# A hybrid encoder with gathered experts: buffers of the prompt's routing moved off the gather ring's space, the first ids at raised priority, norm products on ScalarE and POOL

## The chip, the cores and the metric

The kernel runs on one core of a Trainium2 chip. The metric is the device time of one execution in microseconds (us); less is better. The kernel before takes 4287.37 us, the median of three runs (4286.51 to 4300.59).

## What is computed

One encoder layer is applied with the same weights to two groups of tokens: the prompt (1 x 256 tokens) and the sample (1 x 1024 tokens), each of width 1024. Cut to what matters here:

```python
h = rmsnorm(x, norm_mix)                       # the "norm" of this case
parts = split(h @ w_in)                        # the projection
y_h = hgrn2_branch(...) @ w_br_h
y_a = mla_branch(...) @ w_br_a
x = x + (sigmoid(gl_h) * y_h + sigmoid(gl_a) * y_a) @ w_out    # the merge
z = rmsnorm(x, norm_ffn)
# PEER: 8 heads, 128 x 128 experts, 16 chosen per head
q = (z @ peer_wq) -> (token, head, 2, 128)
vals, idx = top_k(q . sub_keys, 16)            # per half of the key
top, pos = top_k(sums of the 16 x 16 pairs, 16)
g = softmax(top); e = ids of the chosen experts
act = gelu(z . peer_u[e]) * g                  # 128 rows of 1024 per token
x = x + sum(act * peer_v[e])                   # 128 rows of 1024 per token
y = rmsnorm(x, norm_final)
```

All data are float32. The two tables `peer_u` and `peer_v` have 16384 rows of 1024 each.

## The kernel before

Tokens lie in tiles of 128. The prompt has two tiles, the sample eight. The program goes through the prompt's projection, scan and attention first; then through the norm of the sample (its first step); then through the prompt's `merge`; and then through the sample's projection, scan, attention and merges. For six tiles (two of the prompt, four of the sample) the experts' rows are gathered from DRAM; for the other four of the sample all 16384 experts are multiplied densely on PE, at the end of the program.

The work of the sample's norm is in `project` (L204), loop L212 to L221. For each tile of 128 tokens it loads `xt` (L214), takes the sum of squares (`norm_T`, L187 to L201, squares on ScalarE, the sum over partitions on PE, L198, and the root on ScalarE and DVE, L165 to L171) into `nr`, and then for each of 8 slices of the width makes `hf` = xt x gain x nr in one operation on DVE (L218). `put` (L154) splits it in two parts for PE: ScalarE casts `hh` (L159), DVE subtracts `hl` = hf - hh (L160). `hf` has three buffers. The projection (`block`, `proj`, L138 to L142) multiplies each weight block first with tokens 0 to 511 of the sample and then with tokens 512 to 1023; each matmul is done as three (hh x wh, hl x wh, hh x wl).

The prompt's `merge` (L699) combines the branches, adds x, stores the new rows to `x2d` (L762), and then for 16 blocks of query weights `wq` (j = 0 to 15, L138 with `xg`) copies the result (`qT`, ScalarE, L867), multiplies it with the keys on PE (L871), and takes the best 16 of each on DVE (`best`, L849 to L857). After j = 7 the heads 0 to 3 of a tile have all scores: `half(c, 0)` (L812) makes their 64 ids `ei` (L845). `finish_picks` (after the loop) makes the other half.

The gathers are in `experts`, `u_steps` (L928) and `v_steps` (L951). `u_steps` loads the tile's rows `zs` (on POOL's queue, L931), multiplies by the norm (L934), and then for each of 128 choices gathers 128 rows of `peer_u` (512 KB, issued by POOL, L938) and multiplies them with `zs` on DVE, with the sum over a row kept (L940). `v_steps` gathers rows of `peer_v` (L969), and PE adds four of them at a time to `acc` (L976, 8 matmuls). The gathers go through a ring of seven buffers (`ring`, L925) in a pool that is opened at L1166, together with `zt`, set to zero by POOL at L1169.

Each pool is on the left or the right side of the on-chip memory, and pools of a side are stacked: a pool opened later on the right takes the place of pools closed before. On the right, `wpp` (L1137), the prompt's weight pool, stays open through the prompt's merge, and the merge puts its own pool C (`xg`, `qT`, `ssq`, L710) on the right too; the ring's pool comes after both.

The order of instructions on each engine is fixed when the program is built: a scheduler runs through the program with its own estimates of durations and issues what is ready, by priority; `tc.high_priority()` raises that of the instructions made inside it. On the chip each engine executes its list in order, with semaphores between engines. POOL's list has the gathers, SP's the plain loads and stores.

Of the kernel before, what the change touches and what calls it, by code (L numbers as in the profile page):

```python
# [12 lines left out]
F32 = mybir.dt.float32  # L13
# [5 lines left out]
AF = mybir.ActivationFunctionType  # L19
OP = mybir.AluOpType  # L20
# [22 lines left out]
G_MIX, G_FFN, G_QA, G_KVA, G_HG = 0, 8, 16, 19, 21  # L43
# [7 lines left out]
def encoder(ctx, tc, I, O, dbg=None):  # L51
    nc = tc.nc
# [5 lines left out]
    vsp = vctx.enter_context(tc.tile_pool(name="vs", bufs=1, side="left"))  # L58
    wctx = ctx.enter_context(ExitStack())
    wp = wctx.enter_context(tc.tile_pool(name="wp", bufs=2, side="left"))  # L60
# [6 lines left out]
    gains = const.tile([P, 25], F32, name="gains")  # L67
# [83 lines left out]
        return (pool.tile(shape, F32R, name=name + "h", **{k: v + "h" if k == "tag" else v for k, v in kw.items()}),  # L151
                pool.tile(shape, F32R, name=name + "l", **{k: v + "l" if k == "tag" else v for k, v in kw.items()}))

    def put(dst, src):  # L154

        if len(dst) == 1:
            nc.scalar.copy(dst[0], src)
        else:
            nc.scalar.copy(dst[0], src)  # L159
            nc.vector.tensor_tensor(dst[1], src, dst[0].bitcast(F32), op=OP.subtract)  # L160

    def rsqrt_to(pool, out, src, inv_n, shape, name, vy=None):

# [40 lines left out]
    def project(s0, S, ap, wpool, bank, np_, whole):  # L204
# [5 lines left out]
        H = parts(ap, [P, KD, S], "h", whole)  # L210
        ns = 256 if whole else 128
        for t0 in range(0, S, ns):  # L212
            xt = np_.tile([P, KD, ns], F32, name="xt", tag="xt", bufs=256 // ns)
            nc.sync.dma_start(xt, I["xT"][:, :, s0 + t0:s0 + t0 + ns])  # L214
            r = norm_T(np_, [xt[:, k] for k in range(KD)], KD, ns, "nA", bank, whole)
            for k in range(KD):
                hf = H[0][:, k, t0:t0 + ns] if whole else np_.tile([P, ns], F32, name="hf", tag="hf", bufs=3)
                nc.vector.scalar_tensor_tensor(out=hf, in0=xt[:, k], scalar=gains[:, G_MIX + k:G_MIX + k + 1],  # L218
                                               in1=r, op0=OP.mult, op1=OP.mult)
                if not whole:  # L220
                    put([a[:, k, t0:t0 + ns] for a in H], hf)  # L221
        yield

        def stage():
# [471 lines left out]
        nc.vector.tensor_tensor(j, j, last, op=OP.add)  # L696
        return i, j

    def merge(s0, t0, G, nd, routes, wpool, rp, bank, wb=3, small=False, tbank=None, tside="left", tctx=None, cut=0, sp=None, mp=None):  # L699

        with ExitStack() as own, ExitStack() as cctx:
# [3 lines left out]
            segs = [(a, b) for a, b in ((0, ndt), (ndt, G)) if a < b]  # L707
            if not nd:
                cp = own.enter_context(tc.tile_pool(name=f"T{s0}_{t0}", bufs=1, side=tside))
            ca = cctx.enter_context(tc.tile_pool(name=f"C{s0}_{t0}", bufs=1, side="right"))  # L710
            xs = [ca.tile([P, KD, b - a], F32, name=f"xg{a}") for a, b in segs]
            rt = rp.tile([P, ng], F32, name="rt", tag="rt", bufs=4)
            ssq = ca.tile([P, G], F32, name="ssq")
# [145 lines left out]
            for j in range(16):  # L859
# [15 lines left out]
                    norm()  # L875
                if j == 7:
                    for c in range(nd or 1):
                        half(c, 0)
            if nd:
                for k in range(KD):  # L880
                    z = ca.tile([P, ndt], F32, name="z", tag="qT0", bufs=2)
# [243 lines left out]
    def psum_pool(ctx, name, n, side):  # L1125
        pool = ctx.enter_context(tc.tile_pool(name=name, bufs=n, space=bass.MemoryType.PSUM, side=side))
        return lambda: pool.tile([P, 512], F32, name="pm", tag="pm")

    (p0, PS), (s0, SS) = SEQS
    routes = []  # L1130
    rp = ctx.enter_context(tc.tile_pool(name="rp", bufs=1, side="right"))
# [2 lines left out]


    with ExitStack() as pctx:
        wpp = pctx.enter_context(tc.tile_pool(name="wpp", bufs=1, side="right"))  # L1137
        with ExitStack() as qctx:
            bankA = psum_pool(qctx, "psA", 2, "right")
            bankB = psum_pool(qctx, "psB0", 2, "right")  # L1140
            bankT = psum_pool(qctx, "psT0", 1, "right")
# [20 lines left out]
        prs = project(s0, SS, ap, wp, bankF, np_, False)  # L1162
        next(prs)
        with ExitStack() as mctx:
            merge(p0, 0, PS, 0, routes, wpp, rp, psum_pool(mctx, "psM0", 4, "right"), small=True, cut=1, sp=wp, mp=vsp)
    pe_ = ctx.enter_context(tc.tile_pool(name="peer", bufs=1, side="right"))  # L1166
    zts.append(pe_.tile([P, 2, 4, 4, 32], F32, name="zt0"))
    for z_ in zts:
# [51 lines left out]
    tctx = ExitStack()  # L1220
# [95 lines left out]
```

## Time and profile before

| | |
|---|---|
| three runs, median (lowest to highest) | 4287.37 us (4286.51 to 4300.59) |
| the profiled execution's own time | 4300.6 us |
| its span, first to last instruction | 4298.8 us |
| PE, DVE, ScalarE (ACT), POOL busy | 88%, 75%, 36%, 42% |
| moved by DMA | 1263.92 MB, mean 294 GB/s |
| mean granted clock of PE | 0.941 |

PE is TensorE, PEld its weight loads, DVE VectorE, ACT ScalarE, POOL GpSimd, SP SyncE. A row of a timeline gives start, length, engine, line, operation, output and input, and in brackets how long the engine had been idle and what it waited for. A row of waits gives the total in us, the number of times, and the longest. A row of a stretch gives the busy us of each engine and, in brackets, its instructions. The profiled execution is the one of 4300.6 us, the slowest of the three.

### The profile page before, as it was taken

Reading aid. Unit: us, or ns where it says so; the run is one execution under the profiler, and the core shown is the slowest. Engines: PE = TensorE matmul, PEld = TensorE weight load, DVE = VectorE, ACT = ScalarE, POOL = GpSimd, SP = SyncE. Lnnn points to the kernel's source line nnn. Section 1 sums busy time; section 2 is a strip of 40 time slices with the busy share of each in tenths; the row PEclk is TensorE's granted clock in tenths of the full one; section 3 lists DMA queues with packets and bytes.
Section 4 is the critical chain, followed back from the end, with each engine's and each line's share of the span. In section 5 each row is a group of like instructions: output and inputs, shape, how many; then the busy total and the mean of one; then the engine's idle time right before and its main releaser. Section 6 shows DMA issues by size and latency. Waiting matters only on the chain.

```text
span 4298.8 us, 55005 instructions
## 1 busy us (share of the span) xinstructions
PE 3802.2 (88%) x18206; PEld 2734.5 (64%) x18206; DVE 3234.1 (75%) x8002; ACT 1559.9 (36%) x2600; POOL 1818.6 (42%) x1565
## 2 busy tenths in 40 slices
PE   6998999997777988877988489999999999899998
PEld 5777777775434753345644155677777877777786
DVE  4637988567988773986679985567668999999954
ACT  5555455454233214431201187522222222222232
POOL 0000644334444343774545512344446556666500
PEclk9999999998888999888999688999999999999999
DMA  5455899889999987998988847899999999999941
GB/s 160 123 183 152 324 344 343 315 305 319 318 311 313 323 312 272 328 339 326 334 293 285 292 181 292 325 322 339 334 333 356 339 358 362 365 364 346 326 140 64
DMA packets 508318, 1263.92 MB, mean 294 GB/s; under 512 B 49920, under 2 KB 203136, under 8 KB 505984
## 3 DMA queue, kind: packets, MB, share of 16 engines
q0 software_dynamic: 224352, 816.94, 52.9%
q1 hardware_dynamic: 197056, 354.05, 24.2%
q10 hardware_dynamic: 86624, 89.40, 6.1%
q8 instruction: 144, 2.36, 0.2%
q14 instruction: 142, 1.16, 0.1%
HBM read 1165.05 MB, written 95.16 MB: 293 GB/s over the span
## 4 chain that ended last, share of the span: by engine, by line
PE 55%; DMA 13%; DVE 12%; issue 12%; ACT 4%; POOL 2%; SPq 0%; another core or an unknown queue 0%; POOLq 0%; ACTq 0%; DVEq 0%
PE pm L140 12%; PE pm L141 11%; PE pm L142 11%; PE pm L138 7%; DMA vg<-peer_v,eit 5%; PE acc L976 5%; DVE ug L940 4%; DMA ug<-peer_u,ei 3%; PE pm L1053 3%; POOL ug L938 1%; PE pm L1034 1%; PE pm L437 1%; DVE vacc L996 1%; POOL vg L969 1%; PE pm L624 1%
## 5 line engine op out<-in xcount | busy, mean ns | idle before, releaser
L938 POOL DMA_INDIRECT ug<-peer_u,ei x768 | 908.9, 1184 | 800.8 <-DVE ug L940 334.2
L940 DVE SCALAR_TENSOR_TENSOR ug<-ug,zs 128x1024 f32<-128x1024 f32 x768 | 931.5, 1220 | 252.6 <-DMA ug<-peer_u,ei 189.3
L969 POOL DMA_INDIRECT vg<-peer_v,eit x512 | 540.7, 1056 | 752.8 <-DVE ug L940 308.9
L994 POOL DMA_INDIRECT vg<-peer_v,ei x256 | 354.7, 1385 | 207.0 <-DVE vacc L996 120.3
L141 PE MATMUL pm<-vl,ah 128*128 128x512 f32 x1024 | 405.1, 397 | 22.8 <-DVE vl L124 22.8
L140 PE MATMUL pm<-zth,uh 128*128 128x512 f32 x1024 | 406.3, 397 | 8.7 <-ACT ge L1080 6.0
L142 PE MATMUL pm<-zth,ul 128*128 128x512 f32 x1024 | 405.2, 396 | 0.0
L141 PE MATMUL pm<-ztl,uh 128*128 128x512 f32 x1024 | 404.8, 395 | 0.0
L976 PE MATMUL acc<-vg,zt 128*32 128x512 f32 x2048 | 284.6, 679 | 133.7 <-DMA vg<-peer_v,eit 132.8
L142 PE MATMUL pm<-vh,al 128*128 128x512 f32 x1024 | 400.6, 394 | 0.0
L140 PE MATMUL pm<-vh,ah 128*128 128x512 f32 x1024 | 374.9, 398 | 11.3 <-DVE acc L1096 5.5
L996 DVE SCALAR_TENSOR_TENSOR vacc<-vg,act,vacc 128x1024 f32<-128x1024 f32 x256 | 327.7, 1280 | 3.0 <-DMA vg<-peer_v,ei 0.9
L138 PE MATMUL pm<-xg,wraw 128*128 128x256 f32 (+1 forms) x1024 | 295.2, 441 | 4.1 <-DVE sr L855 4.1
L123 ACT CAST uh<-uraw 128x1024 fp32r<-128x1024 f32 x128 | 134.5, 1051 | 432.5 <-PE pm L141 413.2
L123 ACT CAST vh<-vraw 128x512 fp32r<-128x512 f32 x256 | 157.5, 618 | 352.0 <-DMA vraw<-peer_v 257.3
L140 PE MATMUL pm<-hh,wh 128*128 128x512 f32 x672 | 269.9, 402 | 5.0 <-ACT gt L240 3.0
L141 PE MATMUL pm<-hl,wh 128*128 128x512 f32 x672 | 268.3, 399 | 0.0
L142 PE MATMUL pm<-hh,wl 128*128 128x512 f32 x672 | 266.3, 396 | 0.0
L138 PEld LDWEIGHTS pm<-xg,wraw 128*128 128x128 f32 x1024 | 193.2, 194 | 80.6 <-issue 56.9
L141 PEld LDWEIGHTS pm<-vl,ah 128*128 128x128 f32 x1024 | 194.0, 189 | 75.1 <-DVE vl L124 31.5
L140 PEld LDWEIGHTS pm<-vh,ah 128*128 128x128 f32 x1024 | 194.1, 190 | 66.4 <-DVE acc L1096 14.1
L140 PEld LDWEIGHTS pm<-zth,uh 128*128 128x128 f32 x1024 | 192.2, 188 | 64.6 <-ACT ge L1080 11.4
(368 smaller groups left out, 7502.1 us busy)
## 6 DMA issues: line engine op xcount, KB each, us to landing
uraw<-uT SPq DMA_DIRECT2D x128, 512.0 KB
vraw<-peer_v SPq DMA_DIRECT2D x256, 256.0 KB
wraw<-wi SPq DMA_DIRECT2D x84, 512.0 KB
gd<-gs ACTq DMA_DIRECT2D x16, 2048.0 KB
g<-gd ACTq DMA_DIRECT2D x32, 1024.0 KB
wraw<-wq SPq DMA_DIRECT2D x48, 512.0 KB
wraw<-wo SPq DMA_DIRECT2D x24, 512.0 KB
ug<-peer_u,ei POOLq DMA_INDIRECT x768
```

The lines of the kernel that those rows point to most:

```text
L123: nc.scalar.copy(hi, src)
L138: nc.tensor.matmul(out, w[0], x[0], start=start, stop=stop)
L140: nc.tensor.matmul(out, w[0], x[0], start=start, stop=False)
L141: nc.tensor.matmul(out, w[0], x[1], start=False, stop=False)
L142: nc.tensor.matmul(out, w[1], x[0], start=False, stop=stop)
L938: nc.gpsimd.indirect_dma_start(out=ug, out_offset=None, in_=I["peer_u"], in_offset=bass.IndirectOffsetOnAxis(ap=ei[:, s:s + 1], axis=0))
L940: nc.vector.scalar_tensor_tensor(out=ug, in0=ug, scalar=1.0, in1=zs, op0=OP.mult, op1=OP.mult, accum_out=dots[:, s:s + 1])
L969: nc.gpsimd.indirect_dma_start(out=vg, out_offset=None, in_=I["peer_v"], in_offset=bass.IndirectOffsetOnAxis(ap=eit[:, t:t + 1], axis=0))
L976: nc.tensor.matmul(acc[g_ * 32:(g_ + 1) * 32, n * 512:(n + 1) * 512], zt[:, h, g_, i], v_[:, n * 512:(n + 1) * 512], start=b == 0 and i == ...
L994: nc.gpsimd.indirect_dma_start(out=vg, out_offset=None, in_=I["peer_v"], in_offset=bass.IndirectOffsetOnAxis(ap=ei[:, s:s + 1], axis=0))
L996: nc.vector.scalar_tensor_tensor(out=acc, in0=vg, scalar=act[:, s:s + 1], in1=acc, op0=OP.mult, op1=OP.add)
L1053: nc.tensor.matmul(pm[:, j * P:(j + 1) * P], ol[:, j], oh[:, j], start=True, stop=True)
```

## The change

It does three things. First, the prompt's weight pool `wpp` is closed with the prompt's attention; the prompt's merge takes its weights from `wp`, the pool on the left side that also feeds the sample's projection (three raw buffers in rotation), and its pool C is put on the left. Nothing of the prompt's routing is then left on the right when the ring's pool is opened. Second, the first half of the first tile's ids is made at raised priority. Third, in the sample's norm the product on DVE is split: ScalarE multiplies by the gain, POOL by `nr`; and the difference `hl` goes from DVE to POOL.

```diff
--- before.py
+++ after.py
@@ -151,13 +151,13 @@
         return (pool.tile(shape, F32R, name=name + "h", **{k: v + "h" if k == "tag" else v for k, v in kw.items()}),
                 pool.tile(shape, F32R, name=name + "l", **{k: v + "l" if k == "tag" else v for k, v in kw.items()}))
 
-    def put(dst, src):
+    def put(dst, src, eng=None):
 
         if len(dst) == 1:
             nc.scalar.copy(dst[0], src)
         else:
             nc.scalar.copy(dst[0], src)
-            nc.vector.tensor_tensor(dst[1], src, dst[0].bitcast(F32), op=OP.subtract)
+            (eng or nc.vector).tensor_tensor(dst[1], src, dst[0].bitcast(F32), op=OP.subtract)
 
     def rsqrt_to(pool, out, src, inv_n, shape, name, vy=None):
 
@@ -215,10 +215,13 @@
             r = norm_T(np_, [xt[:, k] for k in range(KD)], KD, ns, "nA", bank, whole)
             for k in range(KD):
                 hf = H[0][:, k, t0:t0 + ns] if whole else np_.tile([P, ns], F32, name="hf", tag="hf", bufs=3)
-                nc.vector.scalar_tensor_tensor(out=hf, in0=xt[:, k], scalar=gains[:, G_MIX + k:G_MIX + k + 1],
-                                               in1=r, op0=OP.mult, op1=OP.mult)
-                if not whole:
-                    put([a[:, k, t0:t0 + ns] for a in H], hf)
+                if whole:
+                    nc.vector.scalar_tensor_tensor(out=hf, in0=xt[:, k], scalar=gains[:, G_MIX + k:G_MIX + k + 1],
+                                                   in1=r, op0=OP.mult, op1=OP.mult)
+                else:
+                    nc.scalar.activation(out=hf, in_=xt[:, k], func=AF.Copy, scale=gains[:, G_MIX + k:G_MIX + k + 1])
+                    nc.gpsimd.tensor_tensor(hf, hf, r, op=OP.mult)
+                    put([a[:, k, t0:t0 + ns] for a in H], hf, nc.gpsimd)
         yield
 
         def stage():
@@ -696,7 +699,7 @@
         nc.vector.tensor_tensor(j, j, last, op=OP.add)
         return i, j
 
-    def merge(s0, t0, G, nd, routes, wpool, rp, bank, wb=3, small=False, tbank=None, tside="left", tctx=None, cut=0, sp=None, mp=None):
+    def merge(s0, t0, G, nd, routes, wpool, rp, bank, wb=3, small=False, tbank=None, tside="left", tctx=None, cut=0, sp=None, mp=None, cside="right"):
 
 
 
@@ -707,7 +710,7 @@
             segs = [(a, b) for a, b in ((0, ndt), (ndt, G)) if a < b]
             if not nd:
                 cp = own.enter_context(tc.tile_pool(name=f"T{s0}_{t0}", bufs=1, side=tside))
-            ca = cctx.enter_context(tc.tile_pool(name=f"C{s0}_{t0}", bufs=1, side="right"))
+            ca = cctx.enter_context(tc.tile_pool(name=f"C{s0}_{t0}", bufs=1, side=cside))
             xs = [ca.tile([P, KD, b - a], F32, name=f"xg{a}") for a, b in segs]
             rt = rp.tile([P, ng], F32, name="rt", tag="rt", bufs=4)
             ssq = ca.tile([P, G], F32, name="ssq")
@@ -875,7 +878,10 @@
                     norm()
                 if j == 7:
                     for c in range(nd or 1):
-                        half(c, 0)
+                        with ExitStack() as hctx_:
+                            if not nd:
+                                hctx_.enter_context(tc.high_priority())
+                            half(c, 0)
             if nd:
                 for k in range(KD):
                     z = ca.tile([P, ndt], F32, name="z", tag="qT0", bufs=2)
@@ -1134,8 +1140,8 @@
 
 
     with ExitStack() as pctx:
-        wpp = pctx.enter_context(tc.tile_pool(name="wpp", bufs=1, side="right"))
         with ExitStack() as qctx:
+            wpp = qctx.enter_context(tc.tile_pool(name="wpp", bufs=1, side="right"))
             bankA = psum_pool(qctx, "psA", 2, "right")
             bankB = psum_pool(qctx, "psB0", 2, "right")
             bankT = psum_pool(qctx, "psT0", 1, "right")
@@ -1162,7 +1168,7 @@
         prs = project(s0, SS, ap, wp, bankF, np_, False)
         next(prs)
         with ExitStack() as mctx:
-            merge(p0, 0, PS, 0, routes, wpp, rp, psum_pool(mctx, "psM0", 4, "right"), small=True, cut=1, sp=wp, mp=vsp)
+            merge(p0, 0, PS, 0, routes, wp, rp, psum_pool(mctx, "psM0", 4, "right"), small=True, cut=1, sp=wp, mp=vsp, cside="left")
     pe_ = ctx.enter_context(tc.tile_pool(name="peer", bufs=1, side="right"))
     zts.append(pe_.tile([P, 2, 4, 4, 32], F32, name="zt0"))
     for z_ in zts:
```

Over the whole program DVE has 128 instructions less, ScalarE 64 more and 7 table loads more, POOL 128 more. PE and SP have as many as before; the places of instructions shift on every engine.

Two places show it. The first is POOL's list where the gathers begin (`zs` the tile's rows, `ug` a gather, `hf` and `hl` the norm's products). Before:

```order
masks.py:199 AFFINE_SELECT ident<-ident 128x128
L1169 MEMSET zt_3898 128x1024
L931 DMA zs<-x2d 128x1024
L938 DMA ug<-peer_u,ei 128x1024 x129
L969 DMA vg<-peer_v,eit 128x1024
```

Now, from the last products ahead of the first gather on (lines of the changed file: L223 is the product, L944 the gather):

```order
L160 TENSOR_TENSOR hl<-hf,hh 128x128 x3
L944 DMA ug<-peer_u,ei 128x1024 x7
L223 TENSOR_TENSOR hf<-hf,nr 128x128 x3
L944 DMA ug<-peer_u,ei 128x1024 x2
L160 TENSOR_TENSOR hl<-hf,hh 128x128 x3
L944 DMA ug<-peer_u,ei 128x1024 x2
L223 TENSOR_TENSOR hf<-hf,nr 128x128 x2
L944 DMA ug<-peer_u,ei 128x1024
L160 TENSOR_TENSOR hl<-hf,hh 128x128 x2
L944 DMA ug<-peer_u,ei 128x1024 x4
L223 TENSOR_TENSOR hf<-hf,nr 128x128 x3
L944 DMA ug<-peer_u,ei 128x1024
```

The memset and the load of `zs` now stand ahead of the products of tiles 4 to 8, and the gathers stand between the products of the last two tiles: 22 gathers are ahead of the last `hl`.

The second is DVE's list at the first product of a gather (`L940` before, `L946` now). Before, it stands after the last of the 32 top-16 steps (`L853` to `L857`) and after the last `hl`:

```order
L856 MAX vals<-sr 128x8
L160 TENSOR_TENSOR hl<-hf,hh 128x128
L819 CAST idb<-idxs 128x128
L934 SCALAR_TENSOR_TENSOR zs<-zs,rt,gffn 128x1024
L673 MAX tops<-cd 128x8 x3
L857 MAX_INDEX idxs<-vals,sr 128x8
L673 MAX tops<-cd 128x8
L940 SCALAR_TENSOR_TENSOR ug,dots<-ug,zs 128x1024
```

Now it stands after 25 of these 32 steps (`L856` to `L860`), which go on between the products:

```order
L857 MAX_INDEX idxs<-vals,pm 128x8
L858 MATCH_REPLACE sr<-vals,pm 128x128
L946 SCALAR_TENSOR_TENSOR ug,dots<-ug,zs 128x1024
L860 MAX_INDEX idxs<-vals,sr 128x8
L859 MAX vals<-sr 128x8
L860 MAX_INDEX idxs<-vals,sr 128x8
L946 SCALAR_TENSOR_TENSOR ug,dots<-ug,zs 128x1024
L856 MAX vals<-pm 128x8
L857 MAX_INDEX idxs<-vals,pm 128x8
L858 MATCH_REPLACE sr<-vals,pm 128x128
L856 MAX vals<-pm 128x8
L946 SCALAR_TENSOR_TENSOR ug,dots<-ug,zs 128x1024
```

The cast to `ei` stands after 23 of the 32 steps now and after 27 before; from the start of the half's candidates to it there are 99 instructions now and 138 before.

## Rows read from the trace of the kernel before

**Rows 1.** The page, its part 1: busy time of each engine, share of the span.

```profile
PE 3802.2 (88%) x18206; PEld 2734.5 (64%) x18206; DVE 3234.1 (75%) x8002; ACT 1559.9 (36%) x2600; POOL 1818.6 (42%) x1565
```

**Rows 2.** Stretches: length, PE, PEld, DVE, ACT, POOL busy, clock, DMA share, GB/s.

```profile
285.00:352.00 67.00, 59.42 (x378) 54.22 (x377) 43.16 (x121) 47.58 (x119) 0.00 (x0) 0.95 0.70 217
352.00:391.00 39.00, 34.29 (x167) 29.68 (x167) 26.29 (x154) 15.60 (x44) 0.00 (x0) 0.91 0.42 127
391.00:437.00 46.00, 38.42 (x191) 32.73 (x189) 41.96 (x250) 18.34 (x51) 0.00 (x0) 0.96 0.31 90
437.00:500.00 63.00, 60.30 (x256) 49.12 (x257) 59.95 (x218) 25.82 (x38) 46.17 (x34) 0.95 0.94 339
500.00:1000.00 500.00, 479.31 (x2287) 378.02 (x2286) 364.72 (x789) 255.65 (x345) 223.90 (x191) 0.98 0.92 330
1000.00:1400.00 400.00, 291.63 (x1495) 174.61 (x1494) 340.69 (x914) 138.84 (x270) 183.32 (x174) 0.83 0.91 313
1400.00:2200.00 800.00, 676.07 (x3553) 410.91 (x3552) 569.41 (x1727) 228.31 (x477) 418.02 (x373) 0.92 0.90 317
2200.00:2500.00 300.00, 197.51 (x809) 97.18 (x808) 267.05 (x1274) 44.36 (x73) 142.33 (x139) 0.82 0.81 278
2500.00:4100.00 1600.00, 1541.97 (x7121) 1161.06 (x7120) 1293.90 (x1963) 575.26 (x841) 801.99 (x647) 0.99 0.91 331
```

**Rows 3.** Waits of PE: in 285 to 440, 1000 to 2200, 2200 to 2500 us.

```profile
PE pm L871 <- ACT qT L867: 13.1, 5, 4.3
...
PE acc L976 <- DMA vg<-peer_v,eit: 58.3, 31, 6.1
...
PE acc L976 <- DMA vg<-peer_v,eit: 72.7, 13, 14.9
```

**Rows 4.** Timeline of POOL from 427 us: start, length, operation, wait before it.

```profile
438.74 0.95 POOL L1169 MEMSET zt<- 128x1024 f32 x1 [437.42 <-PE pm L871]
...
440.63 1.07 POOL L938 DMA_INDIRECT ug<-peer_u,ei  x1 [0.30 <-DVE vals L853]
...
450.69 1.47 POOL L938 DMA_INDIRECT ug<-peer_u,ei  x1 [0.30 <-issue]
...
452.47 1.20 POOL L938 DMA_INDIRECT ug<-peer_u,ei  x1 [0.30 <-issue]
```

**Rows 5.** Timeline of DVE, 395 to 448 us.

```profile
396.40 0.38 DVE L665 TENSOR_TENSOR cd<-vals 128x224 f32<-128x224 f32 x1
...
429.04 0.18 DVE L845 CAST ei<-ids 128x64 int32<-128x64 f32 x1
...
443.21 0.28 DVE L160 TENSOR_TENSOR hl<-hf,hh 128x128 fp32r<-128x128 f32 x1
...
444.32 1.28 DVE L934 SCALAR_TENSOR_TENSOR zs<-zs,rt,gffn 128x1024 f32<-128x1024 f32 x1 [0.70 <-DMA zs<-x2d]
...
446.38 1.20 DVE L940 SCALAR_TENSOR_TENSOR ug<-ug,zs 128x1024 f32<-128x1024 f32 x1
```

**Rows 6.** Timeline of PE, 434 to 448 us.

```profile
437.40 1.23 PE L871 MATMUL pm<-kj,qT 128*128 128x128 f32 x4 [2.71 <-ACT qT L867]
...
438.27 0.77 PE L140 MATMUL pm<-hh,wh 128*128 128x512 f32 x1
...
446.35 0.39 PE L140 MATMUL pm<-hh,wh 128*128 128x512 f32 x1
```

**Rows 7.** Groups by line, DVE and ACT, 285 to 445 us: busy, mean ns, idle before.

```profile
L218 DVE SCALAR_TENSOR_TENSOR hf<-xt,gains,nr 128x128 f32<-128x128 f32 x64 | 19.8, 345 | 0.2
...
L160 DVE TENSOR_TENSOR hl<-hf,hh 128x128 fp32r<-128x128 f32 x64 | 16.9, 284 | 0.0
...
L159 ACT CAST hh<-hf 128x128 fp32r<-128x128 f32 x64 | 17.7, 295 | 28.6 <-DVE hf L218 27.5 <-DVE sr L855 1.1
...
L166 ACT ACT_TABLE_LOAD x8 | 10.3, 1283 | 0.1
```

## The prediction

> **What bounds the kernel now.** I read the busy times first, then the same by stretch, then what PE waits for, and last the timeline of 395 to 453 us, where the change lies. PE is busy 3802.2 us of 4298.8 [rows 1]; every other engine has more slack. By stretch [rows 2] the kernel falls in three. From 437 to 1000 us and from 2500 to 4100 us PE is busy 95 to 96% of the time: there only PE's own work or a stall of PE changes the end. From 1000 to 2500 us PE is idle about 335 us (291.63 of 400, 676.07 of 800, 197.51 of 300 busy), DVE is busy 85%, 71% and 89%, and PE's largest wait is for gathered rows of the value table, 58.3 us in 31 waits up to 2200 us and 72.7 us in 13 after that [rows 3]: here gathers done earlier are worth something. From 352 to 437 us, ahead of the first gather, DMA is busy 42% and then 31% (127 and 90 GB/s) against 81 to 94% and 278 to 339 GB/s after it [rows 2]. That hole is what the change can fill.
>
> The first gather is issued at 440.63 [rows 4]. Its ids (`ei`, L845) are written at 429.04 [rows 5], 11.6 us before: so the ids do not hold it. POOL's memset of `zt`, which opens the ring's space, starts at 438.74, when PE's last score matmul (L871, 437.40) has let go of the prompt's routing buffers [rows 4, 6]. Space is the first bound and the ids the second, and the change moves both.
>
> **The change part by part.** *Space and ids.* With the ring's space free, the first gather waits for the ids alone. Between the start of the half's candidates (396.40) and `ei` (429.04) DVE issues 138 instructions in the order before and 99 in the new one; at the old pace, 32.6/138 = 0.236 us each, 99 take 23.4 us, so `ei` comes at 419.8 from the same start. DVE is also relieved ahead of that start, but it was idle a third of 352 to 391 us [rows 2], so the start was mostly not its doing: I give this 3 us, and take 417 for the first gather (ends 413, with 7 us, and 429, with the ids as before). That is 23.6 us earlier. Seven gathers take 452.47 - 440.63 = 11.84 us, 1.69 each [rows 4]: 14 gathers come forward into the hole.
>
> What becomes of a lead of 14? From 437 to 1000 us PE is the bound and the instruction order on every engine fixes how many gathers lie between two steps. Counted over the two listings, what remains at the step that runs at about 1000 us is 5 gathers of the first table on DVE and 4 of the second on PE, so 9. At the second merge (2200 to 2480 us) it is 2 or none. So the lead is paid out between 1000 and 2200 us, in the stretch that gathers and DVE bound. Five products of DVE (1.20 us and some [rows 5]) fewer there are 6.3 us at a DVE that is 85% busy: **-5.5**, ends 0 and -6.3. Four gathers less to wait for, at 400/174 = 2.30 us each, the pace of POOL's rows from 1000 to 1400 us [rows 2], are 9.2 us, of which I take half, since PE waits there for other things as often: **-5**, ends 0 and -9.2. After 2200 us: **-3**, ends 0 and -5, for two products that DVE has less when it is 89% busy. Together -13.5.
>
> *Products off DVE.* DVE loses 64 products (L218, 19.8 us) and 64 differences (L160, 16.9 us) [rows 7], 36.7 us in 285 to 443 us. What does PE gain by it? Its largest wait there is 13.1 us for ScalarE's copy of the queries [rows 3], and not for DVE. So I take **-2** (ends -5 and 0): the rest of the relief is already in the earlier `ei`.
>
> *Products onto ScalarE.* 64 more activations of 128x128 at about 0.30 us, as the casts of `hh` (17.7 us for 64 [rows 7]), are 18 us. From 285 to 352 us ScalarE is busy 47.58 of 67 us [rows 2], and the copies of queries that PE waits for lie behind the new ones in its order: **+3**, ends 0 and +6. The seven added table loads (1.283 us each [rows 7]) lie after 437 us, where ScalarE is half idle: 0, and +9 if each met PE.
>
> *Products onto POOL.* No row shows a POOL product. The nearest are POOL's memset of 128x1024, 0.95 us [rows 4], eight times the elements, and DVE's 128x128 product, 19.8/64 = 0.31 us [rows 7]. I take 0.3, nearer in work; ends 0.12 (the memset by size) and 0.95. POOL is idle up to 437 us [rows 2], so 128 x 0.3 = 38 us cost nothing by themselves. Their place in the queue does: the last two tiles' products stand among the first 22 gathers, each queued behind a gather that needs a ring buffer. At 417 us + 22 x 1.69 = 454 us the last `hl` is out, and some 1 us later it is written; before it was at 443.21 + 0.28 [rows 5]. PE needs it at 446.35, when the projection turns to tokens 512 to 1023 [rows 6], and PE executes in order, so everything behind it waits: 455.5 - 446.35 = 9.2, **+9**, ends 0 (PE has moved later by as much through ScalarE) and +20 (0.95 us per product, on the last 16 alone 10 us more). From 437 us on PE is the bound, so this is paid in full.
>
> The prefetch of the first two projection blocks is lost: their load now stands behind the last query weights. 512 KB at 339 GB/s [rows 2] are 1.5 us, and the first of their buffers comes free two blocks of query weights before the projection: 0, end +5.
>
> **Sum**: -13.5 - 2 + 3 + 9 = -3.5. On the profiled execution, 4300.6 us, that is 4297.1; this one is the slowest of the three and 13.2 us above the median of 4287.37, so by the median **4284**. About 0.5% (21 us) is what a measurement of this kernel can tell from no change: the forecast is no change that can be told.
>
> **Rivals.**
> *A, the lead is worth its full length.* From 437 to 4100 us the DMA engines are busy 81 to 94% in every stretch [rows 2]. If transfers set the end and not PE, 14 gathers moved into the hole at 2.30 us are -32 us, and no more than the 23.6 us by which they begin earlier. PE's stall is then covered by the transfers: 4287.4 - 23.6 - 2 + 3 = **4265**. For it: the gap ahead of 437 us and the 131 us of waits for gathered rows. Against it: PE at 96% from 2500 us, and a lead that the listings show gone by the second merge. Chance 0.25.
>
> *B, the projection stalls* (the other sign). Each gather in the queue ahead of tile 8's products waits for a ring buffer that DVE frees; DVE's product stands behind top-16 steps that wait for scores of PE, which wait for ScalarE's copies, and ScalarE's casts wait for POOL's products. With that loop 22 gathers take 3 us each instead of 1.69, the last `hl` comes at 417 + 66 = 483 us, and PE stalls 37 us. With 13.5 of gains and 3 for ScalarE: +26, **4313**. It decides from a stall of about 33 us on; for it speaks that PE's last score matmul waited 2.71 us for ScalarE's copy already [rows 6]; against it, that gathers need only DVE's 1.2 us each to free a buffer. Chance 0.15.
>
> *C, the change doesn't do what it says.* Something else holds the first gather to 435 us or later: the product of `zs` (444.32, after a wait for its load [rows 5]), which needs rows stored by the merge, or POOL's products of tiles 4 to 7 ahead of it in the queue, which wait for the norm. Then the gains are 0 and the costs half: +6, **4293**. Chance 0.15.
>
> *D, POOL and DVE keep each other out.* The products that leave DVE come back to it as waits: 128 products of POOL at 0.3 us block two-input operations of DVE for up to 38 us, as much as the 36.7 us removed. Then `ei` stays near 429, the first gather comes 11 us earlier instead of 24, the gains halve to -7, and with +3 and +7 for the stall the sum is +3: **4290**. The rows before show nothing on this: from 285 to 437 us POOL is not busy at all [rows 2]. The Trainium skill's page "SBUF — State Buffer" (section "Who interferes with whom") states this rule: VectorE and GpSimd share a port pair, and an operation of VectorE with two inputs in SBUF and one of GpSimd that reads SBUF do not overlap; the second waits for the end of the first. By that rule D is the case; no row here shows it yet. Chance 0.15.
>
> **How the numbers follow.** My forecast, 0.30 (the gains and stall about as priced, 4270 to 4298); A 0.25; B 0.15; C 0.15; D 0.15. A lies at the edge of -0.5% (4266), so half or a little more of it counts as faster, 0.16, and with a tail of the forecast where the stall is 0 and all gains come (-20 us), 0.10: 0.26. Slower by 0.5% (over 4309): two thirds of B, and parts of C where the stall is whole and nothing is gained (+17 to +25): 0.16. Same: 0.58. The range leaves out the lowest third of A (below 4258) and half of B (above 4311).
>
> **What would show it.** Right: the first gather at 413 to 422 us, DMA's share from 417 to 437 us up from 31% to over 60%; POOL's products 0.2 to 0.4 us; the last `hl` at about 455 us and PE waiting 5 to 15 us for it at the projection's second half; first-table products on DVE ending about 20 us earlier, and waits for gathered rows from 1000 to 2200 us some 5 to 10 us shorter. Wrong: for A, time before the second merge shorter by over 20 us; for B, a wait of PE over 30 us between 440 and 490 us; for C, a first gather after 430 us; for D, DVE's two-input operations longer or gapped beside POOL's products, and `ei` no earlier than 427. The sum is wrong if PE's stall is not paid (PE's later stretches absorb it) or if the new order of instructions costs PE a wait somewhere that no row of before shows.

## The result and the profile after

The changed kernel takes 4318.35 us, the median of four runs (4314.46 to 4326.62), against 4286.94 us before (4285.91 to 4300.59): a ratio of the mean times of 1.0068 with a 95% interval of 1.0042 to 1.0095, or some 29 us (18 to 41). The forecast was 4284 us and no change; the time lies above the range of 4258 to 4311.

The profiled execution has a span of 4324.8 us, 26.0 more than before. The page's part 1:

```profile
PE 3812.9 (88%) x18206; PEld 2746.0 (63%) x18206; DVE 3214.9 (74%) x7874; ACT 1590.7 (37%) x2671; POOL 1858.3 (43%) x1693
```

DVE has lost 19 us of work and POOL gained 40, and the kernel is slower. Where it loses is seen by comparing the start of the same matmul in both traces (the n-th of a line with the n-th): PE is 0.9 us early at 263 us, 4.3 late at 430, **24.6 late at 480**, 32.6 at 857, 19.8 at 2159 and 26.1 at the last matmul of the dense part. Most of the loss arises within 50 us and is never made up. (Behind that, the lag depends on the execution that one compares with: against e9, another profile of the kernel before, it is 24.9 us at 480 and 47.7 at 4100.) By stretches, the columns of [rows 2]:

```profile
352.00:391.00 39.00, 33.43 (x164) 28.89 (x163) 22.96 (x120) 22.43 (x65) 15.12 (x34) 0.91 0.51 153
...
391.00:437.00 46.00, 38.37 (x201) 33.24 (x199) 36.60 (x198) 22.24 (x59) 19.49 (x32) 1.00 0.53 172
...
437.00:500.00 63.00, 50.09 (x176) 38.20 (x177) 56.13 (x192) 28.09 (x49) 47.02 (x52) 0.81 0.85 302
...
500.00:1000.00 500.00, 471.90 (x2225) 371.73 (x2224) 352.36 (x770) 255.29 (x338) 215.76 (x182) 0.98 0.90 320
...
1000.00:1400.00 400.00, 299.31 (x1539) 180.14 (x1537) 338.79 (x901) 150.91 (x283) 179.84 (x175) 0.86 0.91 312
...
2200.00:2500.00 300.00, 199.17 (x812) 100.68 (x814) 256.27 (x1221) 34.61 (x59) 145.67 (x140) 0.83 0.80 275
```

From 391 to 437 us DMA is now busy 53% instead of 31%, so the hole is filled. From 437 to 500 us PE is busy 50.09 us instead of 60.30, at a mean granted clock of 0.81 instead of 0.95, with 176 matmul rows instead of 256; the stretches after it differ by some us each. POOL's timeline there:

```profile
422.22 1.37 POOL L223 TENSOR_TENSOR hf<-hf,nr 128x128 f32<-128x128 f32 x3 [16.37 <-DVE nr L171]
...
425.17 1.02 POOL L944 DMA_INDIRECT ug<-peer_u,ei  x1 [0.34 <-DVE ei L848]
...
435.30 2.27 POOL L223 TENSOR_TENSOR hf<-hf,nr 128x128 f32<-128x128 f32 x3
...
437.73 0.97 POOL L944 DMA_INDIRECT ug<-peer_u,ei  x1 [0.16 <-issue]
...
455.68 1.01 POOL L944 DMA_INDIRECT ug<-peer_u,ei  x1 [2.80 <-DVE idxs L860]
...
456.71 2.43 POOL L223 TENSOR_TENSOR hf<-hf,nr 128x128 f32<-128x128 f32 x3
...
474.81 1.43 POOL L160 TENSOR_TENSOR hl<-hf,hh 128x128 fp32r<-128x128 f32 x1 [0.24 <-ACT hh L159]
```

The first gather is issued at 425.17, 15.5 us earlier than in [rows 4], but the products stand between the gathers, and three of them take 2.27 and 2.43 us there instead of 1.37. By the 25th gather the lead is 479 against 484 us, and the 128th is 6 us later than before (753 against 747). DVE, with the ids and the last tile's norm (L165 to L171):

```profile
400.87 0.58 DVE L668 TENSOR_TENSOR cd<-vals 128x224 f32<-128x224 f32 x1
...
424.41 0.47 DVE L848 CAST ei<-ids 128x64 int32<-128x64 f32 x1
...
431.25 1.22 DVE L946 SCALAR_TENSOR_TENSOR ug<-ug,zs 128x1024 f32<-128x1024 f32 x1 [3.04 <-DMA ug<-peer_u,ei]
...
435.47 1.79 DVE L946 SCALAR_TENSOR_TENSOR ug<-ug,zs 128x1024 f32<-128x1024 f32 x1
...
439.53 0.27 DVE L165 TENSOR_SCALAR nAv<-pm 128x128 f32<-128x128 f32 x1
...
444.97 1.42 DVE L124 TENSOR_TENSOR wl<-wraw,wh 128x1024 fp32r<-128x1024 f32 x1 [2.83 <-ACT wh L123]
...
447.46 0.53 DVE L168 TENSOR_TENSOR nAv<-nAv,nAy 128x128 f32<-128x128 f32 x1
...
455.61 0.27 DVE L171 TENSOR_TENSOR nr<-nAv,nAy 128x128 f32<-128x128 f32 x1
```

The ids come 23.5 us after the start of the half's candidates, which starts at 400.87 and not at 396.40. The last tile's norm begins at 439.53 (430.54 before) and ends with `nr` at 455.61. Nine gather products stand ahead of this `nr` on DVE, four before 439.53 and five after it, and in between DVE stands idle for 2.83 us until ScalarE has cast a weight block (`wh`). Before, the `nr` of the last two tiles were at:

```profile
416.65 0.28 DVE L171 TENSOR_TENSOR nr<-nAv,nAy 128x128 f32<-128x128 f32 x1
...
435.94 0.28 DVE L171 TENSOR_TENSOR nr<-nAv,nAy 128x128 f32<-128x128 f32 x1
```

The first seven tiles' `nr` are 3.4 to 5.8 us later than before (the seventh at 421.86), and the eighth's is 19.7 us later: the jump comes with the first gathers. ScalarE waits for POOL:

```profile
435.80 0.71 ACT L159 CAST hh<-hf 128x128 fp32r<-128x128 f32 x2 [5.23 <-POOL hf L223]
...
441.27 0.82 ACT L222 ACTIVATE hf<-xt,gains 128x128 f32<-128x128 f32 x2 [3.10 <-POOL hl L160]
...
443.40 0.31 ACT L166 ACTIVATE nAy<-nAv 128x128 f32<-128x128 f32 x1
...
446.66 0.36 ACT L870 COPY qT<-pm 128x256 f32<-128x256 f32 x1
```

The copy of the last queries, which PE's last score matmul needs, stands in ScalarE's list behind an activation that waits 3.10 us for a buffer (a difference on POOL, behind gathers, must release it) and behind the late norm's table loads. Over 285 to 480 us, by line:

```profile
L222 ACT ACTIVATE hf<-xt,gains 128x128 f32<-128x128 f32 x61 | 23.9, 399 | 8.1 <-POOL hl L160 7.0
...
L159 ACT CAST hh<-hf 128x128 fp32r<-128x128 f32 x64 | 18.5, 293 | 30.0 <-POOL hf L223 28.6
```

PE waits for all of it. These are the rows that answer to [rows 6]:

```profile
447.07 1.22 PE L874 MATMUL pm<-kj,qT 128*128 128x128 f32 x4 [2.99 <-ACT qT L870]
...
447.95 0.77 PE L140 MATMUL pm<-hh,wh 128*128 128x512 f32 x1
...
458.29 0.74 PE L140 MATMUL pm<-hh,wh 128*128 128x512 f32 x2 [2.23 <-ACT hh L159]
...
468.73 0.50 PE L141 MATMUL pm<-hl,wh 128*128 128x512 f32 x1 [0.81 <-POOL hl L160]
...
474.63 0.79 PE L141 MATMUL pm<-hl,wh 128*128 128x512 f32 x1 [1.19 <-POOL hl L160]
...
480.14 0.80 PE L140 MATMUL pm<-hh,wh 128*128 128x512 f32 x1 [2.62 <-ACT gt L258]
```

The last score matmul starts at 447.07 instead of 437.40. Then the projection waits for `hh` and `hl` five times, and 2.62 us for ScalarE's activation behind them: 8.7 us in all. The last `hl` is written at 476.2 us; before it was 443.5.

### The profile page after: what moved, and what is told of

Its sections match the earlier page's. It is cut to its first block, busy times and chain, and to the rows that moved or that the text cites. A ratio compares the mean times of both kernels' runs of the same rounds, so it can differ in the third digit from the quotient of the medians.

```text
span 4324.8 us, 55058 instructions
## 1 busy us (share of the span) xinstructions
PE 3812.9 (88%) x18206; PEld 2746.0 (63%) x18206; DVE 3214.9 (74%) x7874; ACT 1590.7 (37%) x2671; POOL 1858.3 (43%) x1693
## 4 chain that ended last, share of the span: by engine, by line
PE 39%; DMA 9%; issue 9%; DVE 6%; POOL 3%; ACT 1%; SPq 0%; POOLq 0%; another core or an unknown queue 0%; DVEq 0%; ACTq 0%
PE pm L140 9%; PE pm L142 9%; PE pm L141 9%; PE pm L138 4%; PE acc L982 4%; DMA vg<-peer_v,eit 4%; DMA ug<-peer_u,ei 3%; PE pm L1059 3%; POOL ug L944 2%; DVE ug L946 2%; PE pm L1040 1%; DVE vacc L1002 1%; POOL vg L975 1%; PE pm L627 1%; DMA g<-gd 1%
## 5 line engine op out<-in xcount | busy, mean ns | idle before, releaser
L944 POOL DMA_INDIRECT ug<-peer_u,ei x768 | 913.2, 1189 | 849.6 <-DVE ug L946 319.5
L946 DVE SCALAR_TENSOR_TENSOR ug<-ug,zs 128x1024 f32<-128x1024 f32 x768 | 932.1, 1221 | 283.0 <-DMA ug<-peer_u,ei 249.0
L1000 POOL DMA_INDIRECT vg<-peer_v,ei x256 | 331.2, 1294 | 244.5 <-DVE vacc L1002 172.4
L140 PE MATMUL pm<-vh,ah 128*128 128x512 f32 x1024 | 384.5, 399 | 10.5 <-ACT vh L123 5.3
L142 PEld LDWEIGHTS pm<-zth,ul 128*128 128x128 f32 x1024 | 192.9, 188 | 56.9 <-DVE ul L124 5.7
```

Of the source, the lines that this page charges most:

```text
L140: nc.tensor.matmul(out, w[0], x[0], start=start, stop=False)
L142: nc.tensor.matmul(out, w[1], x[0], start=False, stop=stop)
L944: nc.gpsimd.indirect_dma_start(out=ug, out_offset=None, in_=I["peer_u"], in_offset=bass.IndirectOffsetOnAxis(ap=ei[:, s:s + 1], axis=0))
L946: nc.vector.scalar_tensor_tensor(out=ug, in0=ug, scalar=1.0, in1=zs, op0=OP.mult, op1=OP.mult, accum_out=dots[:, s:s + 1])
L1000: nc.gpsimd.indirect_dma_start(out=vg, out_offset=None, in_=I["peer_v"], in_offset=bass.IndirectOffsetOnAxis(ap=ei[:, s:s + 1], axis=0))
```

## The experiments

Ratios are against runs of the kernel before on the same chip. *nr* is the start of the last operation of the last tile's norm (L171), *hl* the end of the last difference, *PE at 480* how much later the matmul runs that is at 479.9 us in the trace of e9 (for the change, against the profile of before; a minus is earlier).

| run | what | nr, us | hl, us | first gather | PE at 480 | ratio (95%) |
|---|---|---|---|---|---|---|
| change | | 455.6 | 476.2 | 425.2 | +24.6 | 1.0068 (1.0042 to 1.0095) |
| e1 | norm on DVE | 428.2 | 443.0 | 429.5 | -0.7 | 1.0036 (1.0018 to 1.0053) |
| e2 | norm's part alone | 451.1 | 478.8 | 436.7 | +27.5 | 1.0083 (1.0059 to 1.0108) |
| e3 | last two tiles on DVE | 454.3 | 473.8 | 425.7 | +23.2 | 1.0104 (1.0077 to 1.0131) |
| e5 | space alone | 432.9 | 447.0 | 434.5 | +2.8 | 1.0016 (1.0001 to 1.0030) |
| e6 | change, eight buffers | 431.2 | 439.3 | 446.5 | +8.3 | 1.0030 (1.0017 to 1.0044) |
| e7 | only hl on POOL | 444.1 | 460.5 | 428.7 | +8.7 | 1.0039 (1.0024 to 1.0053) |
| e8 | e2, eight buffers | 441.5 | 455.7 | 448.5 | +8.8 | 1.0036 (1.0021 to 1.0051) |
| e9 | before again | 435.9 | 442.9 | 440.1 | 0 | |
| e10 | e1 + 1 POOL product | 429.4 | 443.3 | 431.0 | +0.6 | 1.0051 (1.0032 to 1.0070) |
| e11 | e1 + 48 POOL products | 431.7 | 446.7 | 433.3 | +9.4 | 1.0097 (1.0076 to 1.0117) |
| e12 | change, reordered | 449.1 | 469.7 | 418.9 | +18.7 | 1.0064 (1.0040 to 1.0089) |
| e13 | before, 12 memsets | 434.9 | 441.9 | 439.0 | -1.9 | 0.9978 (0.9962 to 0.9993) |
| e14 | before, 8 memsets | 434.4 | 441.9 | 439.0 | +1.3 | 1.0025 (1.0010 to 1.0041) |
| e15 | before, 16 memsets | 433.6 | 441.1 | 438.3 | -2.2 | 0.9971 (0.9958 to 0.9985) |
| e16 | before, 32 memsets | 432.9 | 440.4 | 437.6 | -3.5 | 1.0065 (1.0042 to 1.0087) |
| e17 | e1 + 1 small product | 431.4 | 445.7 | 433.0 | +2.7 | 1.0020 (1.0007 to 1.0034) |

The four versions that are 18 us or more late at 480 lie at 1.0064 to 1.0104; those less than 10 us late lie at 0.9971 to 1.0051, but for e11 and e16, which are taken up below.

**First: which part loses.** e1 takes the norm back to DVE and keeps the rest:

```diff
-                    nc.scalar.activation(out=hf, in_=xt[:, k], func=AF.Copy, scale=gains[...])
-                    nc.gpsimd.tensor_tensor(hf, hf, r, op=OP.mult)
-                    put([a[:, k, t0:t0 + ns] for a in H], hf, nc.gpsimd)
+                    put([a[:, k, t0:t0 + ns] for a in H], hf)
```

> Space freed and ids at raised priority as in the change, the sample's norm products on DVE as before. Theory Q (the products stand behind ring gathers in POOL's queue, ScalarE's casts wait for them, and PE's last score matmul and the projection's second half wait for both): the loss is gone, last score matmul at 437 +-3 us, last hl by 448 us, 4275 to 4290 us. Theory A (the loss is ScalarE's added work): the loss is gone too, 4275 to 4290. Theory E (gathers that begin early are the loss, since their products stand on DVE ahead of the last top-16 steps and the weights' differences): still slow, last score matmul at 442 or later, 4300 to 4320.

The projection's loss is gone, so gathers that begin early do not make it (theory E falls). But nothing is gained either: its median of 4290.6 us is just above the range expected and 13 us above that of the kernel before on the same chip.

e2 is the kernel before with the three lines the other way round (the `-` lines in, DVE's out), e3 the change with `if whole or t0 >= 768:` ahead of DVE's form, e5 is e1 without the raised priority.

> The kernel before with the norm products on ScalarE and POOL alone; the ring's space is not freed, so gathers begin where they did or later. The list of POOL has 12 gathers ahead of the last tile's differences. Theory Q: the last score matmul is near 437 to 442 us (no gathers ahead of it), but the last hl comes 10 to 20 us after 443, PE stalls for it; 4295 to 4310. Theory A: 4305 to 4320, with the delay already there at the last score matmul (446 or later). Theory E: no loss, 4280 to 4295.

> The change, with the products of the last two of the sample's eight tiles back on DVE: no product stands behind a gather in POOL's list. Theory Q: the loss is gone, last hl by 450 us, 4275 to 4292. Theory A: most of the loss stays (48 of 64 added activations remain), 4303 to 4318. Theory E: the loss stays, 4300 to 4320.

> The space freed alone: ids at ordinary priority, norm on DVE. First gather at 429 to 433 us instead of 440.6, six gathers brought forward. Theory Q: 4278 to 4290, and if a lead is worth 1 us per gather, some 6 below before. Theory E: 4290 to 4305.

e2 loses 27.5 us at 480 though its gathers begin only 3.4 us earlier than in e9; its last `hl` comes 36 us later, where theory Q had 10 to 20. DVE, then POOL:

```profile
451.08 0.29 DVE L171 TENSOR_TENSOR nr<-nAv,nAy 128x128 f32<-128x128 f32 x1
```

```profile
436.69 1.01 POOL L941 DMA_INDIRECT ug<-peer_u,ei  x1 [0.30 <-issue]
...
455.49 2.28 POOL L223 TENSOR_TENSOR hf<-hf,nr 128x128 f32<-128x128 f32 x3
...
478.33 0.49 POOL L160 TENSOR_TENSOR hl<-hf,hh 128x128 fp32r<-128x128 f32 x1
```

Its last score matmul (first row) is earlier than before, against theory A, and in e5, with the norm on DVE, it is at 442.97 (second row). (The gathers of e5 begin at 434.5 and not by 433 as expected, and it gains nothing: 1.0016.)

```profile
433.92 0.71 PE L874 MATMUL pm<-kj,qT 128*128 128x128 f32 x4
```

```profile
442.97 0.71 PE L871 MATMUL pm<-kj,qT 128*128 128x128 f32 x4 [1.65 <-ACT qT L867]
```

So a later last score matmul doesn't need the norm's products: part of it comes with the freed space.

e3 contradicts theory Q as I had put it. No product stands behind a gather on POOL there, and PE still loses 23.2 us, since the last tile's norm and its products now stand among the gathers' products on DVE:

```profile
454.30 0.29 DVE L171 TENSOR_TENSOR nr<-nAv,nAy 128x128 f32<-128x128 f32 x1
...
473.51 0.27 DVE L160 TENSOR_TENSOR hl<-hf,hh 128x128 fp32r<-128x128 f32 x1
```

What the change, e2 and e3 share is the late `nr`, 451 to 456 us. So the theory became N: the norm's tiles come later, tile by tile, through the loop ScalarE, POOL, ScalarE, POOL on three buffers of `hf`, and the last falls behind the gathers in whatever list it stands.

**Second: theory N.** e6 changes one number of the change, e8 the same in e2; e7 keeps DVE's one operation and gives POOL the difference alone.

```diff
-np_.tile([P, ns], F32, name="hf", tag="hf", bufs=3)
+np_.tile([P, ns], F32, name="hf", tag="hf", bufs=8)
```

> The whole change, with eight buffers for the norm's product instead of three. By the list of instructions all products and the last tile's norm then stand ahead of the first gather on POOL and of its product on DVE. Theory N (the loop of the product through ScalarE and POOL on three buffers makes the last tile's norm late, so that it falls among the gathers' products and the gathers; the projection's second half waits for it): the last tile's norm factor at 430 +-4 us instead of 455.6, last hl by 445, PE's projection not stalled, ratio to before 0.997 to 1.004. Theory A (ScalarE's added work and table loads by themselves): ratio 1.005 or more, the last score matmul still at 443 or later.

> The change with the product left on DVE in one operation and only the difference hl on POOL, three buffers; ScalarE gets nothing. By the list the last tile's norm factor stands after 4 gather products on DVE (9 in the change) and its hl behind 12 gathers on POOL (14 to 22 in the change). Theory N: a smaller loss, norm factor at 440 to 446, last hl at 455 to 465, stall of PE 8 to 15 us, ratio 1.003 to 1.007. Theory A: no loss, ratio 0.998 to 1.003, since ScalarE has no work added.

> The norm's part of the change alone (the space is not freed, ids at ordinary priority), with eight buffers. Theory N: no loss, last hl at 445 to 450, ratio 0.997 to 1.003. Theory A: ratio 1.005 or more. Beside the whole change with eight buffers it gives what gathers that begin 10 to 15 us earlier are worth: by the prediction's price some 13 us, by what the runs so far show 0 or a few us lost.

In e6 POOL makes a tile's eight products and then its eight differences in one go, 0.42 and 0.54 us each, all ahead of the gathers:

```profile
431.63 3.34 POOL L223 TENSOR_TENSOR hf<-hf,nr 128x128 f32<-128x128 f32 x8 [12.11 <-DVE nr L171]
...
434.93 4.33 POOL L160 TENSOR_TENSOR hl<-hf,hh 128x128 fp32r<-128x128 f32 x8
...
446.51 1.02 POOL L944 DMA_INDIRECT ug<-peer_u,ei  x1 [0.30 <-issue]
```

ScalarE hardly waits for buffers any more (L222, 0.6 us idle instead of 8.1):

```profile
L222 ACT ACTIVATE hf<-xt,gains 128x128 f32<-128x128 f32 x57 | 20.6, 394 | 0.6 <-POOL hl L160 0.2
```

`nr` is at 431.2 and the last `hl` at 439.3, earlier than before; ScalarE's added work is all there, and the ratio of 1.0030 is under theory A's 1.005. PE's 8.3 us at 480 come with a last score matmul at 443.7 us; theory A foretold that too, but e5's is at 443.0 without any work added to ScalarE. e6 is not a gain: by the order the scheduler chose, its first gather comes at 446.5. e7 lies between, as expected of N. e8 missed N's figures: last `hl` at 455.7 (445 to 450 expected), PE 8.8 us late, 1.0036 (at most 1.003). Its gathers begin 2 us after those of e6, so the two don't price an earlier start.

One part of N does not hold: the norm does not come later and later, tile by tile. The last two `nr` of e8:

```profile
421.84 0.27 DVE L171 TENSOR_TENSOR nr<-nAv,nAy 128x128 f32<-128x128 f32 x1
...
441.46 0.27 DVE L171 TENSOR_TENSOR nr<-nAv,nAy 128x128 f32<-128x128 f32 x1
```

The seventh is as late as in the change (421.86), the eighth 14 us earlier than there: in e8 no gather product stands ahead of it. What these runs show is that a last norm among the gathers or their products is enough for the stall (e2 and e3), and that without it most of the stall is gone (e1, e6, e8). Eight buffers changed two things at once, ScalarE's waits and the order that the scheduler made; which of the two keeps the norm ahead of the gathers is not shown.

e9 is the kernel before, for a profile on this chip:

> The kernel before, unchanged, for a profile on the chip of these runs: the same as before within 0.5%, its first gather near 440 us and the last tile's norm factor near 436 us.

It gave 4278.92 us, first gather 440.1.

**Third: what the gathers' timing is worth.** e10 and e11 add to e1 one and 48 small POOL products on the first ids:

```diff
+            with tc.high_priority():
+                for _ in range(48):
+                    nc.gpsimd.tensor_tensor(hold, e0, e0, op=OP.mult)
```

> Space freed and ids at raised priority, norm on DVE (as e1), with one added POOL product of 64 columns on the first ids. Gathers begin near 430 us; the added operation gives the scheduler another order of the whole program, so this is e1 in another order. If the residue of e1 (ratio 1.0036) comes from the gathers' early start, the ratio is 1.002 to 1.005 again. If it comes from the order that the scheduler happens to give, the ratio may be anywhere from 0.996 to 1.008.

> As e10 but with 48 of these POOL products, one after the other, in POOL's list among the first 25 gathers. The order on PE, DVE, ScalarE and SP is the same as in e10; only POOL's list differs, and the gathers after the sixth come later, by some 10 us at the 25th. If a lead of the gathers is worth its length, e11 is 8 to 12 us (0.002 to 0.003 of the ratio) above e10; if, as the prediction priced it, 1 us per gather, 5 to 7 us; if PE's order makes the lead worthless from 437 to 1000 us, within 2 us.

The order on the four other engines is the same in both. A product alone takes 0.32 us, four of them beside DVE 4.24:

```profile
432.79 0.32 POOL L944 TENSOR_TENSOR hold<-ei 128x64 f32<-128x64 f32 x1 [74.77 <-DVE ei L845]
...
450.51 4.24 POOL L944 TENSOR_TENSOR hold<-ei 128x64 f32<-128x64 f32 x4
```

The 25th gather is issued at 501 instead of 476 us. DVE's wait for gathers (437 to 600 us) in e10, then in e11:

```profile
DVE ug L949 <- DMA ug<-peer_u,ei: 1.7, 2, 0.9
```

```profile
DVE ug L949 <- DMA ug<-peer_u,ei: 16.3, 8, 4.8
```

PE's waits for the projection's gates (`gt`), which DVE and ScalarE make, sum to 16.1 us instead of 4.8 in that stretch. PE is 17.7 us later at 574 us and 17 to 26 us later from there to 2159 us; at the end it is 13.5 in the profiles, and the ratios differ by 0.0046, some 20 us. So these products, which made the 25th gather 25 us later and not 10 as I had expected, cost more than half of that delay. It need not be so: the memsets among the gathers of e13 and e15 below cost nothing.

**Fourth: the rest.** Versions without the projection's loss still lie 0.2 to 0.5% above before. e12 to e17 change the order without changing what is computed; the edit of e12 to e16 is `for _ in range(12):` (8, 16, 32) ahead of the memset of `zt`, of e17 an added product of 8 columns.

> The whole change, with the memset of zt made 12 times on POOL, which stands idle then. The front of the lists is the change's (last tile's norm factor after 9 gather products), what comes later is another order. Theory N: the projection's stall is there again, PE 20 us or more late at 480 us, ratio 1.005 to 1.011. If the loss were only the later order: 0.998 to 1.006.

> The kernel before with the memset of zt made 12 times: the first gather 10.5 us later (451 us) and another order. The norm and the projection are not touched (last hl at 443). If a lead is worth its length: ratio 1.002 to 1.004. If the order of before is a favourable one among many: 1.001 to 1.005, with the gain or loss spread over 1000 to 2500 us. If neither: 0.999 to 1.001.

> The kernel before with the memset of zt made 8 times: another order than e13, the same arithmetic. Theory O (the residue of 0.2 to 0.5% in the versions without a stall is what a change of order alone gives or takes): the ratios of these reorderings of before spread over some 0.005, some above 1. Theory R (the order of before is nothing special and the residue is a cost of the change): all reorderings of before lie between 0.997 and 1.000, all versions with early gathers above 1.001.

> As e13 (the same order on PE) with 16 memsets in place of 12. Both theories: within 0.002 of e13's 0.998, if the order sets the time; if the memsets among the gathers cost time as the 48 products of e11 did, 0.001 to 0.003 above e13.

> The kernel before with 32 memsets of zt, a third order, and some 15 us of POOL's work among the gathers. Theory O: anywhere from 0.996 to 1.006. Theory R: 0.997 to 1.000 plus what the memsets cost.

> e1 (space and ids early, norm on DVE) in a third order, through one added POOL product of 8 columns. Theory O: anywhere from 0.996 to 1.006. Theory R: 1.002 to 1.005, as e1 and e10.

The first gather of e13 does not come later, though I had expected it: eleven of the memsets stand among the gathers. Its ratio lies below all that I had expected. 12 and 16 memsets (one order on PE) are 0.2 to 0.3% faster than none, 8 memsets (another order) 0.25% slower. More added work and less time: that leaves the order, and with it ScalarE's table loads (161 in e13 and e15, 166 in e14, 167 before). e16, at 1.0065, is just beyond theory O's 1.006, and its added work explains little of it: its last memset is at 522 us, and PE is 9 us behind e13 at 1000 us, but 35 us at 1800. So reordering the kernel before can cost nearly as much as the change does, and a ratio alone does not tell the change from an unlucky order; PE's lag at 480 does (e16 is 3.5 us early there). The early versions (1.0016 to 1.0051) and the reordered kernels before (0.9971 to 1.0065) overlap: a cost of the early start up to some 0.3% is neither shown nor excluded. e12 has the change's front and another order behind it, and loses again (18.7 us at 480, just under the 20 expected). e13 and e15 are faster than both kernels, by an order that happened to suit.

## Why the prediction was wrong

**What bounds the kernel, and the hole.** Right: ids and space were the bounds, and DMA's share from 417 to 437 us went from 13% to 65% (over 60% was foretold).

**First gather at 417.** It came at 425.2. The count was exact, 99 instructions in 23.5 us against 23.4; the start was not. I gave it 3 us for DVE's relief, and it came 4.5 us later.

**"The lead is paid out between 1000 and 2200 us", -13.5.** This step failed. The lead was 15.5 us at the first gather, 5 at the 25th, nothing at the 128th: most of it was lost by 470 us, while products stood among the gathers. But where it lived, in e1 (26 us at the 128th gather, 724 against e9's 750), it was gone by the 256th (1358 against 1360) and no time was gained: PE was 8 us early at 1000 us and 1 us late at 2159. The term measured nothing. Counting places in two listings says where instructions stand, not when they run; e14 against e13 shows orders of nearly the same work 0.5% apart.

**Products off DVE, -2.** Nothing came of it; PE's wait for ScalarE's copies went from 13.1 to 14.3 us [rows 3].

**Products onto ScalarE, +3.** PE was 4.3 us late at 430 us. The size was near. The added work alone need not cost it: e6 carries the same work, in another order, and is 4.7 us early there; in the change ScalarE waits 8.1 us for buffers that POOL releases.

**Products onto POOL, 0.3 us each and a stall of +9.** This is the term that decided. A product takes 0.42 to 0.46 us alone, inside the bounds (0.12 to 0.95). Beside DVE's products of gathers it takes 0.76 to 0.81, and DVE's took 1.79 instead of 1.22. PE's waits in the projection sum to 8.7 us, near the 9.2 foretold. But I had put the stall at one place, the last `hl`. Two more came late: ScalarE's copies and so the last score matmul, 9.7 us, of which the freed space brings a part (e5); and the last tile's norm on DVE, whose place in the list behind nine gather products I had not looked at. That makes 18.4 of the 24.6 us at 480. By an estimate from PE's rows, the clock makes some 2.8 of the other 6.2 us: at the lower of its two levels (1.2 and 2.4 GHz) the projection's matmuls start 0.43 us apart instead of 0.23, and 25 do so on the way to that matmul, 11 before (14 x 0.20). All 25 come soon after PE's waits at 447.07, 458.29, 474.63 and 480.14. The rest is not split. These rows show both levels:

```profile
449.37 0.63 PE L140 MATMUL pm<-hh,wh 128*128 128x512 f32 x1
449.80 0.63 PE L141 MATMUL pm<-hl,wh 128*128 128x512 f32 x1
...
453.59 0.39 PE L142 MATMUL pm<-hh,wl 128*128 128x512 f32 x1
453.82 0.40 PE L140 MATMUL pm<-hh,wh 128*128 128x512 f32 x1
```

So the sum failed in two terms. With the lead worth nothing and the rest as priced it gives 4297 us; with 24.6 us in place of the 3 and the 9 and the gains as priced, 4296.5; with 24.6 us and no gains, 4287.4 + 24.6 = 4312, just above the range. The measured loss is some 29 us; what it has beyond 24.6 is within its interval and within what orders differ by.

**The rivals.** B came nearest, at a chance of 0.15 and 4313 us: the loop through ring, DVE, PE, ScalarE and POOL, last `hl` at 476 (483 foretold). Its own sign, a wait of PE over 30 us between 440 and 490 us, did not show: the waits there sum to 11.7 us. It had the loss too large (37) and the gains too large (13.5), and lacked the norm's part, so that its time came out near is in part luck. D was there too, as a part of it: until 437 us DVE still got its relief (36.60 us busy instead of 41.96), and POOL and DVE lengthened each other's operations; but `ei` came at 424.41 and not after 427. The rule of the Trainium skill ("SBUF — State Buffer", "Who interferes with whom") nearly agrees with these rows: three products at 435.30 and DVE's at 435.47 took 2.3 us together, where alone they take 1.37 and 1.22, 2.6 in sum. A and C were not: the gathers did begin earlier, and nothing was gained by it.

What stays open: whether an early start of the gathers costs or gains anything by itself, below the 0.5% and more by which orders alone differ, and whether three buffers or the scheduler's order put the last tile's norm among the gathers.

## What to carry to other kernels

Work moved to an idle engine takes a place in that engine's list, so ask who stands in front of it there, and what loop of small buffers it now closes: with three buffers through two engines and four hops the last tile's norm fell among the gathers, with eight, and the order that the scheduler then made, it did not. Look up the place of the last link on every engine on the path, not on the one that gets the work. Where a scheduler sets the order, reorder the unchanged kernel a few times before a gain or loss of a few tenths of a per cent is put down to an edit.

## What was not expected

Twelve memsets that nobody needs, 0.97 us each among the gathers, made the kernel before 0.22% faster; eight made it 0.25% slower, and thirty-two 0.65%. A POOL product of 128 x 64 takes 0.32 us alone and 1.06 in a group of four beside a busy DVE.
